# A copy buffer of its own for the final state, and reciprocal key norms spread by a product with the identity

## The chip, the core and the metric

The kernel runs on one core of a Trainium2 chip. The number that counts is device time in microseconds (us) of one execution. Before the change three runs gave 2194.7, 2196.6 and 2201.28 us, median 2196.6.

## What is computed

One inference step of a two-layer decoder: 512 prompt tokens and 8 x 4 sample tokens, model width 1024, 16 heads of 64. Layer 0 mixes time with an RWKV-7 recurrence, layer 1 with dilated window attention, and after each stands a gated feed-forward block. All arithmetic is float32; the large products are done as three products of split operands (a rounded part and its rest). Only the recurrence is touched by the change. Cut down to that, the reference is:

```python
kk = heads(k * k_k)
kk = kk / jnp.maximum(jnp.sqrt(jnp.sum(kk * kk, axis=-1, keepdims=True)), 1e-12)
k = k * (1.0 + (a - 1.0) * k_a)
y, S_T = wkv7_scan(rh, heads(decay), kh, vh, -kk, kk * ah, S0)
#   S = S * w + (S @ a) b^T + v k^T ;  y = S @ r      for each token
mean, var = jnp.mean(y, -1, keepdims=True), jnp.mean(jnp.square(y - mean), -1, keepdims=True)
y = ((y - mean) * lax.rsqrt(var + GN_EPS)).reshape(B, T, D) * ln_w + ln_b
bonus = jnp.sum(rh * kh * r_k, axis=-1, keepdims=True) * vh
out = ((y + bonus.reshape(B, T, D)) * g) @ w_o          # S_T, the last state, is an output too
```

## The kernel before

Tokens lie in two groups: group 0 has 288 columns (256 prompt tokens and the 32 sample tokens), group 1 the other 256. Channels lie in eight blocks `m` of 128, each with two heads; `jj` numbers pairs of blocks. The time mixing goes through these stages:

- Projections (`proj_gemm`, from L361): r, k and v. With k the sum of squares of every head and token is formed, and `rk[m]` holds its reciprocal root, one column for each head and block of 128 tokens.
- Preparation of group 0 (`unit_prep`, eight units), with the rest of the r and v projections beside it. In each unit `head_rows` (L126) turns the columns of `rk[m]` into rows: VectorE copies each column 64 times into `hr_e` (one buffer), TensorE transposes `hr_e` (three blocks for group 0, two for group 1; L135), and VectorE multiplies by the result (`kk`). A unit ends with its matrices `G`.
- `inverses`, nearly all VectorE, which waits for the `G` of all units.
- `chain` of group 0 (`scan(0)`), four steps that hand on the state `S`; beside it and after it the preparation of group 1 and the sample recurrences; then `inverses` of group 1.
- `chain` of group 1, whose four results are the tiles `yt`. Beside it the outputs of group 0: `y_norm` and `y_out`. `y_out` takes `bonus`, which lay in DRAM (`bonus_spill`), through the tile `bonus_in`, four buffers.
- `states` (L805): the last state is transposed in two halves, ScalarE copies each into `p_st`, and SyncE stores it to `o_p_wkv`. Then `y_norm` and `y_out` of group 1, and the products with `w_o` (`mm<-y`), where the rest of the kernel begins.

`p_st` carries the tag `y_sq`: it is the same single buffer in which `y_norm` puts the squares of each `yt`. Inside `y_norm` one tile goes through: sum (VectorE), mean taken off (VectorE), squares into `y_sq` (ScalarE), sum of squares `y_var` and its scaling (VectorE), power and product (GpSimd).

The program is written stage by stage, and a scheduler then places the instructions of all stages on each engine's queue; every engine works through its queue in order. So an instruction that waits holds everything behind it on its engine. Instructions issued through `Stream` all carry line 59 in the trace and are told apart by their tiles.

Of the kernel before, what the change touches and what calls it, by code (L numbers as in the profile page):

```python
# [9 lines left out]
F = mybir.dt.float32  # L10
# [11 lines left out]
NA = 288  # L22
# [7 lines left out]
def blocks(n):  # L30
    return (0, 128, 160) if n == NA else (0, 128)
# [41 lines left out]
def split(c, out_hi, out_lo, src, lo_engine, nc=None):  # L73
    (nc or c.nc).scalar.activation(out_hi, src, AF.Copy)  # L74
    lo_engine.tensor_tensor(out_lo, src, out_hi.bitcast(F), OP.subtract)  # L75
# [49 lines left out]

def head_rows(c, r, g, nc):  # L126

    e = c.lp.tile([128, 3, 128], F, name="hr_e", bufs=1)
    n = GRP[g][1]
    nb = len(blocks(n))  # L130
    nc.vector.tensor_copy(e[:, :nb].rearrange("p b (h k) -> p (b h) k", k=64),
                          r[:, 6 * g:6 * g + 2 * nb].unsqueeze(2).to_broadcast([128, 2 * nb, 64]))
    pr = c.pp()
    for j, at in enumerate(blocks(n)):
        nc.tensor.transpose(pr[:, at:at + 128], e[:, j, :], c.ident)  # L135
    return pr[:, :n]


# [251 lines left out]
def side_of(m):  # L390

    return (UP, LO) if m % 2 else (LO, UP)


def unit_prep(c, g, m, b, up, un, G, UV, bonus):
# [37 lines left out]
    if b:  # L433
        nc.gpsimd.memset(ds[:, :, 0:1], 1.0)
        nc.scalar.activation(ds[:, :, 1:5], s4(cl), AF.Exp, scale=-CDEC)
    prk = head_rows(c, c.rk[m], g, nc)
    kk = up.tile([128, NA], F, name="kk", tag="kk", bufs=c.ub)
    nc.vector.scalar_tensor_tensor(kk[:, :n], kS[:, :n], c.col("rwkv_k_k", m), prk, op0=OP.mult, op1=OP.mult)
# [284 lines left out]
def y_out(c, g, jj, yt, ys, yo, bonus, g2, y):  # L723

    nc, a = c.slow[3], c.a
    g0, n = GRP[g]
    pt = c.pp()
    for ch in range(4):
        nc.tensor.transpose(pt[:, 128 * ch:128 * ch + 128], yt[ch][:, 128 * jj:128 * jj + 128], c.ident)
    if g == 0:  # L730
        pk = c.sm()
        for par in range(2):
            x = 64 * ((2 * jj + par) % 4)
            for h in range(2):
                nc.tensor.matmul(pk[64 * h:64 * h + 64, 32 * par:32 * par + 32], ys[jj // 2][:, x:x + 64],
                                 c.pick[:, 32 * h:32 * h + 32], start=True, stop=True, tile_position=(0, 64 * h))
    for par in range(2):
        m = 2 * jj + par
        if bonus is None:
            bn = yo.tile([128, NA], F, name="bonus_in", bufs=4)  # L740
            nc.sync.dma_start(bn, c.bd[:, m])
        else:
            bn = bonus[:, m]
        bp = bn[:, 0:256].rearrange("p (c t) -> p c t", t=64)
        nc.vector.scalar_tensor_tensor(bp, pt.rearrange("p (c t) -> p c t", t=128)[:, :, side_of(m)[1]],
                                       c.col("rwkv_ln_w", m), bp, op0=OP.mult, op1=OP.add)
        if g == 0:
            nc.vector.scalar_tensor_tensor(bn[:, 256:NA], pk[:, 32 * par:32 * par + 32], c.col("rwkv_ln_w", m),
                                           bn[:, 256:NA], op0=OP.mult, op1=OP.add)
        ps = c.pp()  # L750
        nc.tensor.matmul(ps[:, :n], g2[:, m * 128:(m + 1) * 128], c.hg[:, g0:g0 + n], start=True, stop=True)
        t = yo.tile([128, NA], F, name="y_t", bufs=2)
        for src, to in ((slice(256, NA), slice(0, 32)), (slice(0, 256), slice(32, NA)))[g:]:
            to = slice(0, NB) if g else to
            nc.vector.scalar_tensor_tensor(t[:, to], bn[:, src], c.col("rwkv_ln_b", m), ps[:, src], op0=OP.add, op1=OP.mult)
        split(c, y[:, 0, m, :n], y[:, 1, m, :n], t[:, :n], nc.gpsimd, nc)


def rwkv(c, ctx, mx):

    nc, tc, a = c.nc, c.tc, c.a
    with ExitStack() as rx:
# [38 lines left out]
        def outputs(g):  # L801
            for jj in range(4):
                y_out(c, g, jj, st[g]["yt"], ysm, yo, bonus[g], g2, ys[g])

        def states(hb):  # L805
            pt = c.sm()
            for j in range(4):
                nc.tensor.transpose(pt[:, 128 * j:128 * j + 128], c.S[0][:, 4 * hb + j], c.ident)
            so = yo.tile([128, 4, 128], F, name="p_st", tag="y_sq", bufs=1)
            nc.scalar.activation(so, pt.rearrange("p (j k) -> p j k", j=4), AF.Copy)  # L810
            for h in range(2):
                q = slice(64 * h, 64 * h + 64)
                nc.sync.dma_start(a["o_p_wkv"][0, 0, 8 * hb + h:8 * hb + 8:2].rearrange("j v k -> v j k"), so[q, :, q])
# [98 lines left out]
        yo = rx.enter_context(c.pool("yo"))  # L912
# [13 lines left out]
        for hb in range(2):  # L926
            states(hb)
# [723 lines left out]
```

## Time and profile before

| | |
|---|---|
| median of the runs | 2196.6 us |
| the profiled execution | 2200.44 us |
| its span, first to last instruction | 2198.6 us |
| TensorE busy | 2020.5 us (92%) |
| VectorE busy | 1138.7 us (52%) |
| ScalarE busy | 879.1 us (40%) |
| GpSimd busy | 540.1 us (25%) |

TensorE's share is an average. It is close to full from about 520 us on, in the feed-forward blocks and the attention, and lower in the time mixing before that, where the engines wait for one another. The times below are of the profiled execution, counted from the start of its span.

### The profile page before, as it was taken

What the parts mean: (1) busy time and instruction counts of PE and PEld (TensorE: products, weight loads), DVE (VectorE), ACT (ScalarE), POOL (GpSimd) and SP (SyncE); (2) the same over time, 40 slices, a digit from 0 to 9 for tenths busy, and PEclk for the clock granted to TensorE, in tenths of its full rate; (3) what the DMA queues carried; (4) which work ended last, traced back from release to release, by engine and by line L of the source; (5) the groups of instructions that cost most, each with busy time, mean ns of one, the idle gap of its engine ahead of it and who ended that gap; (6) DMA issues with size and microseconds to landing.
All of it is one profiled execution on the core that took longest, in us unless ns stands there. A gap on an engine that the chain in (4) does not pass through costs nothing. (4 is left out here: it accounts for less than half of the span.)

```text
span 2198.6 us, 47990 instructions
## 1 busy us (share of the span) xinstructions
PE 2020.5 (92%) x19190; PEld 1893.1 (86%) x19190; DVE 1138.7 (52%) x2390; ACT 879.1 (40%) x1815; POOL 540.1 (25%) x680
## 2 busy tenths in 40 slices
PE   7998668487999999998999999999999989999998
PEld 6897556376899999998888988888898889999998
DVE  7647867865644343254554544545545553444323
ACT  5446435223544443243333333333334444444333
POOL 5525525254322221021111111111111132212001
PEclk9999879687999999999999999999999899999999
DMA  5266412313333233355444444444445332333323
GB/s 172 84 179 192 127 26 56 78 36 99 110 88 91 83 97 91 107 159 136 124 134 126 129 127 135 134 116 122 137 126 156 95 108 81 94 87 87 94 81 110
DMA packets 432379, 242.53 MB, mean 110 GB/s; under 512 B 40890, under 2 KB 424026, under 8 KB 432026
## 3 DMA queue, kind: packets, MB, share of 16 engines
q1 hardware_dynamic: 432154, 239.45, 38.5%
q8 instruction: 151, 2.47, 0.5%
q14 instruction: 74, 0.61, 0.1%
HBM read 198.42 MB, written 27.57 MB: 103 GB/s over the span
## 5 line engine op out<-in xcount | busy, mean ns | idle before, releaser
L98 PE MATMUL mm<-xn,w_hi 128*128 128x256 f32 (+1 forms) x2688 | 789.3, 294 | 0.0
L99 PE MATMUL mm<-xn,w_hi 128*128 128x256 f32 (+1 forms) x2688 | 786.3, 293 | 0.9 <-DVE xn L75 0.9
L100 PE MATMUL mm<-xn,w_lo 128*128 128x256 f32 (+1 forms) x2688 | 782.0, 291 | 0.0
L75 DVE TENSOR_TENSOR w_lo<-w_raw,w_hi 128x512 fp32r<-128x512 f32 (+1 forms) x575 | 431.8, 752 | 573.4 <-ACT w_hi L74 566.2
L74 ACT ACTIVATE w_hi<-w_raw 128x512 fp32r<-128x512 f32 (+1 forms) x575 | 355.9, 620 | 572.7 <-PE mm L99 506.1
L99 PEld LDWEIGHTS mm<-xn,w_hi 128*128 128x128 f32 x2688 | 511.5, 190 | 5.3 <-issue 2.8
L98 PEld LDWEIGHTS mm<-xn,w_hi 128*128 128x128 f32 x2688 | 510.4, 190 | 5.8 <-issue 0.4
L100 PEld LDWEIGHTS mm<-xn,w_lo 128*128 128x128 f32 x2688 | 510.6, 190 | 3.1 <-issue 3.0
L98 PE MATMUL mm<-act,w_hi 128*128 128x288 f32 (+1 forms) x704 | 201.2, 290 | 1.6 <-ACT y_out L1029 1.6
L99 PE MATMUL mm<-act,w_hi 128*128 128x288 f32 (+1 forms) x704 | 200.5, 289 | 0.0
L100 PE MATMUL mm<-act,w_lo 128*128 128x256 f32 (+1 forms) x704 | 199.4, 289 | 0.0
L1183 POOL TENSOR_TENSOR qk_raw<-qk_raw,rope 128x1088 f32<-128x1088 f32 x24 | 85.9, 3581 | 422.6 <-DMA qk_sw<-qk_raw 343.8
L98 PEld LDWEIGHTS mm<-act,w_hi 128*128 128x128 f32 x704 | 132.5, 190 | 1.7 <-ACT y_out L1029 1.7
L99 PEld LDWEIGHTS mm<-act,w_hi 128*128 128x128 f32 x704 | 132.3, 189 | 0.0
L100 PEld LDWEIGHTS mm<-act,w_lo 128*128 128x128 f32 x704 | 131.3, 189 | 0.0
L147 POOL TENSOR_TENSOR acc<-acc,sq_t 128x288 f32<-128x288 f32 (+1 forms) x56 | 46.1, 823 | 302.4 <-ACT sq_t L146 302.0
L98 PE MATMUL mm<-mx,w_hi 128*128 128x288 f32 (+1 forms) x384 | 113.0, 296 | 3.2 <-ACT p_out L371 1.6
L100 PE MATMUL mm<-mx,w_lo 128*128 128x288 f32 (+1 forms) x384 | 112.2, 295 | 1.7 <-DVE w_lo L75 1.7
L99 PE MATMUL mm<-mx,w_hi 128*128 128x288 f32 (+1 forms) x384 | 112.2, 293 | 0.0
L1268 ACT ACTIVATE scores<-scores,sm_m 128x512 f32<-128x512 f32 (+3 forms) x80 | 50.4, 631 | 71.5 <-DVE sm_m L1267 71.3
L98 PEld LDWEIGHTS mm<-mx,w_hi 128*128 128x128 f32 x384 | 73.3, 191 | 6.1 <-ACT w_hi L74 2.7
L100 PEld LDWEIGHTS mm<-mx,w_lo 128*128 128x128 f32 x384 | 73.1, 191 | 4.6 <-DVE w_lo L75 3.3
(334 smaller groups left out, 3036.5 us busy)
## 6 DMA issues: line engine op xcount, KB each, us to landing
w_raw<-ffn_w_up SPq DMA_DIRECT2D x176, 256.0 KB
w_raw<-attn_w_in SPq DMA_DIRECT2D x144, 256.0 KB
w_raw<-ffn_w_down SPq DMA_DIRECT2D x90, 256.0 KB
w_raw<-rwkv_w_rkv SPq DMA_DIRECT2D x80, 256.0 KB
qk_sw<-qk_raw SPq DMA_DIRECT2D x96, 136.0 KB
cache_k<-cache_k_w SPq DMA_DIRECT2D x96, 128.0 KB
cache_v<-cache_v_w SPq DMA_DIRECT2D x96, 128.0 KB
w_raw<-rwkv_w_o SPq DMA_DIRECT2D x32, 256.0 KB
```

What stands on the lines that cost most here:

```text
L74: (nc or c.nc).scalar.activation(out_hi, src, AF.Copy)
L75: lo_engine.tensor_tensor(out_lo, src, out_hi.bitcast(F), OP.subtract)
L98: nc.tensor.matmul(ps, hi, xhi(i), start=first and i == 0, stop=False)
L99: nc.tensor.matmul(ps, hi, xlo(i), start=False, stop=False)
L100: nc.tensor.matmul(ps, lo, xhi(i), start=False, stop=last and i == len(w) - 1)
L147: nc.gpsimd.tensor_tensor(acc, acc, t[:, :n], OP.add)
L1183: nc.gpsimd.tensor_tensor(raw, raw, c.rope[:, 0:1].to_broadcast([128, 2, NT]), OP.mult)
L1268: nc.scalar.activation(s[:, :w], s[:, :w], AF.Exp, scale=0.125, bias=m[:, 1:2], accum_out=m[:, 2:3])
```

## The change

`head_rows` no longer makes `hr_e`. For each block of 128 tokens and each of the two heads it issues one product, with the column of `rk[m]` read 64 times as the stationary operand and the identity as the moving one, into the 64 partitions of that head. The rows that come out are the same. `p_st` gets a buffer of its own (2 KB in each partition), and `bonus_in` goes from four buffers to two (1152 bytes each).

```diff
 def head_rows(c, r, g, nc):

-    e = c.lp.tile([128, 3, 128], F, name="hr_e", bufs=1)
     n = GRP[g][1]
-    nb = len(blocks(n))
-    nc.vector.tensor_copy(e[:, :nb].rearrange("p b (h k) -> p (b h) k", k=64),
-                          r[:, 6 * g:6 * g + 2 * nb].unsqueeze(2).to_broadcast([128, 2 * nb, 64]))
     pr = c.pp()
     for j, at in enumerate(blocks(n)):
-        nc.tensor.transpose(pr[:, at:at + 128], e[:, j, :], c.ident)
+        for h in range(2):
+            x = 6 * g + 2 * j + h
+            nc.tensor.matmul(pr[64 * h:64 * h + 64, at:at + 128], r[:, x:x + 1].to_broadcast([128, 64]), c.ident,
+                             start=True, stop=True, tile_position=(0, 64 * h))
     return pr[:, :n]
@@ y_out
-            bn = yo.tile([128, NA], F, name="bonus_in", bufs=4)
+            bn = yo.tile([128, NA], F, name="bonus_in", bufs=2)
@@ states
-            so = yo.tile([128, 4, 128], F, name="p_st", tag="y_sq", bufs=1)
+            so = yo.tile([128, 4, 128], F, name="p_st", bufs=1)
```

The scheduler orders the queues anew. From line 136 on, the changed file's line numbers are one less. At three places this is what stands on a queue before and after.

The first place is the end of the chain of group 1. ScalarE, before: the four `yt` tiles of group 1 are `yt_5279` to `yt_5282`, `cp` and `sm` are PSUM tiles, `y_5278` is the input of the products with `w_o`.

```order
L579 ACTIVATE yt_5281<-cp 128x512
L592 ACTIVATE W<-cp 128x256
L599 ACTIVATE UV<-cp 64x512
L579 ACTIVATE yt_5282<-cp 128x512
L810 ACTIVATE p_st<-sm 128x512 x2
L59 ACTIVATE y_sq<-yt_5279 128x512
L59 ACTIVATE y_sq<-yt_5280 128x512
L59 ACTIVATE y_sq<-yt_5281 128x512
L59 ACTIVATE y_sq<-yt_5282 128x512
L59 ACTIVATE y_5278<-y_t 128x256 x8
```

ScalarE at the same place, after; the four tiles are now `yt_5287` to `yt_5290`.

```order
L59 ACTIVATE y_sq<-yt_5287 128x512
L578 ACTIVATE yt_5289<-cp 128x512
L59 ACTIVATE y_sq<-yt_5288 128x512
L591 ACTIVATE W<-cp 128x256
L598 ACTIVATE UV<-cp 64x512
L59 ACTIVATE y_sq<-yt_5289 128x512
L578 ACTIVATE yt_5290<-cp 128x512
L809 ACTIVATE p_st<-sm 128x512
L59 ACTIVATE y_sq<-yt_5290 128x512
L809 ACTIVATE p_st<-sm 128x512
L59 ACTIVATE y_5286<-y_t 128x256 x8
```

Three of the four squares now stand among the last steps of the chain, and the fourth stands between the two state copies. VectorE's queue follows: after the change its rows between the state updates of the third and the fourth step (`S_3666`, `S_3665`) are these.

```order
L613 TENSOR_TENSOR S_3666<-cp,SD 64x8x64 x2
L59 SCALAR_TENSOR_TENSOR yt_5287<-y_sum,yt_5287 128x512
L59 TENSOR_REDUCE y_sum<-yt_5288 128x8
L59 TENSOR_REDUCE y_var<-y_sq 128x8
L59 TENSOR_SCALAR y_var<-y_var 128x8
L59 SCALAR_TENSOR_TENSOR yt_5288<-y_sum,yt_5288 128x512
L590 COPY W<-cp 128x256
L59 TENSOR_REDUCE y_sum<-yt_5289 128x8
L59 TENSOR_REDUCE y_var<-y_sq 128x8
L59 TENSOR_SCALAR y_var<-y_var 128x8
L59 SCALAR_TENSOR_TENSOR yt_5289<-y_sum,yt_5289 128x512
L597 COPY UV<-cp 64x512
```

Behind the last of these stand one more `y_var` with its scaling and then `S_3665`. Before the change one `y_sum` and the two copies `W` and `UV` were all that stood between the two updates.

The second place is SyncE's queue of DMA issues from the end of the preparation on, before and then after.

```order
L914 DMA g_5011<-rwkv_g 128x1024
L741 DMA bonus_in<-bonus_spill 128x288 x4
L701 DMA o_s_wkv<-st 64x4x64 x16
L86 DMA w_raw<-rwkv_w_o 128x4x128 x8
L741 DMA bonus_in<-bonus_spill 128x288 x4
L955 DMA x<-x_spill 128x544 x3
```

```order
L913 DMA g_5019<-rwkv_g 128x1024
L740 DMA bonus_in<-bonus_spill 128x288 x2
L700 DMA o_s_wkv<-st 64x4x64 x16
L86 DMA w_raw<-rwkv_w_o 128x4x128 x8
L740 DMA bonus_in<-bonus_spill 128x288 x6
L954 DMA x<-x_spill 128x544 x3
```

Two loads of `bonus_in` go early instead of four, and six wait in line for a buffer instead of four.

The third place is GpSimd at the last unit of group 0's preparation, before and then after; `th_3117` and `th_3124` are that unit's tile `th`, and `st` is work for the sample recurrences, which come later.

```order
L59 TENSOR_TENSOR BE<-BK,dc 128x512
L59 MEMSET dx 128x4
L59 TENSOR_TENSOR st<-s_BK_2021,s_dend_2025 128x128 x2
L59 TENSOR_TENSOR s_BK_2028<-tk,di 64x8x4
L59 TENSOR_TENSOR st<-s_BK_2021,s_dend_2025 128x128 x2
L59 TENSOR_TENSOR s_BK_2028<-th_2948,di 64x8x4
L59 TENSOR_SCALAR s_V_2030<-in_2952 64x8x4
L59 TENSOR_TENSOR tk<-in_3120,tk 128x288
```

```order
L59 TENSOR_TENSOR BE<-BK,dc 128x512
L59 TENSOR_TENSOR s_BK_2028<-tk,di 64x8x4
L59 TENSOR_TENSOR s_BK_2028<-th_2954,di 64x8x4
L59 TENSOR_SCALAR s_V_2030<-in_2958 64x8x4
L59 TENSOR_TENSOR tk<-in_3127,tk 128x288
L59 TENSOR_TENSOR th_3124<-kk,th_3124 128x288
```

The four `st` products have left this place; they now stand behind the last unit.

## Rows read from the trace of the kernel before

**Rows 1.** The page's first line: span and instructions.

```profile
span 2198.6 us, 47990 instructions
```

**Rows 2.** Windows: start:end, length, busy us (instructions) by engine, TensorE clock, DMA.

```profile
165.00:265.00 100.00, 81.91 (x672) 72.48 (x672) 80.57 (x149) 61.05 (x144) 61.35 (x109) 0.95 0.61 175
...
489.00:520.10 31.10, 10.09 (x39) 7.17 (x40) 12.37 (x28) 6.69 (x13) 14.54 (x13) 0.62 0.26 80
520.10:2198.60 1678.50, 1628.24 (x15131) 1554.42 (x15129) 773.78 (x1681) 651.75 (x1306) 303.90 (x376) 0.98 0.40 113
```

**Rows 3.** Timeline, 488 to 521 us: start, duration, instruction, [idle before <-releaser].

```profile
488.92 0.60 ACT L579 ACTIVATE yt<-cp 128x512 f32<-128x512 f32 x1 [3.15 <-PE cp L577]
489.95 0.60 ACT L810 ACTIVATE p_st<-sm 128x512 f32<-128x512 f32 x1 [0.43 <-PE sm L808]
494.46 0.60 ACT L810 ACTIVATE p_st<-sm 128x512 f32<-128x512 f32 x1 [3.91 <-DMA o_p_wkv<-p_st]
499.72 0.63 ACT L59 ACTIVATE y_sq<-yt 128x512 f32<-128x512 f32 x1 [4.67 <-DMA o_p_wkv<-p_st]
500.38 0.69 DVE L59 TENSOR_REDUCE y_var<-y_sq 128x8 f32<-128x512 f32 x1 [11.18 <-ACT y_sq L59]
501.42 1.94 POOL L59 TENSOR_TENSOR y_var<-y_var,mhalf 128x8 f32<-128x8 f32 x1 [16.87 <-DVE y_var L59]
510.88 2.04 POOL L59 TENSOR_TENSOR yt<-yt,y_var 128x512 f32<-128x512 f32 x2
520.15 0.49 PE L98 MATMUL mm<-y,w_hi 128*128 128x288 f32 x1
```

**Rows 4.** The last state update, and the window between it and the one before.

```profile
482.28:487.80 5.52, 4.22 (x102) 3.78 (x100) 1.81 (x5) 1.57 (x3) 2.11 (x2) 1.00 0.00 0
487.80 1.41 DVE L614 TENSOR_TENSOR S<-cp,SD 64x512 f32<-64x512 f32 x2 [1.97 <-PE cp L607]
```

**Rows 5.** Timeline of VectorE, 464 to 478 us: outputs of group 0 beside the chain.

```profile
464.65 0.64 DVE L59 SCALAR_TENSOR_TENSOR y_t<-bonus_in,par,pp 128x32 f32<-128x32 f32 x2
466.50 0.88 DVE L59 SCALAR_TENSOR_TENSOR bonus_in<-pp,par,bonus_in 128x256 f32<-128x256 f32 x2 [0.32 <-PE pp L729]
469.78 1.39 DVE L614 TENSOR_TENSOR S<-cp,SD 64x512 f32<-64x512 f32 x2 [0.75 <-PE cp L607]
474.82 0.63 DVE L59 SCALAR_TENSOR_TENSOR y_t<-bonus_in,par,pp 128x32 f32<-128x32 f32 x2
477.31 0.88 DVE L59 SCALAR_TENSOR_TENSOR bonus_in<-pp,par,bonus_in 128x256 f32<-128x256 f32 x2
```

**Rows 6.** Timeline: a load of 144 KB issued by SyncE, and who waited for it.

```profile
191.22 0.43 SPq L411 DMA_DIRECT2D in<-rkv_spill  x1
195.10 0.60 PE L446 MATMUL pp<-ca,in 128*64 128x128 f32 x4 [0.89 <-DMA in<-rkv_spill]
```

**Rows 7.** Windows with the instructions of `hr_e` alone: PE, PEld and DVE busy.

```profile
165.00:265.00 100.00, 4.25 (x24) 2.77 (x24) 4.02 (x8) 0.95 0.61 175
265.00:400.00 135.00, 3.36 (x16) 1.74 (x16) 2.80 (x7) 0.87 0.18 42
```

**Rows 8.** Timeline, 248 to 252 us: last unit of group 0's preparation.

```profile
248.51 1.32 POOL L59 TENSOR_TENSOR st<-s_BK,s_dend 128x128 f32<-128x128 f32 x2
250.00 0.75 POOL L59 TENSOR_TENSOR st<-s_BK,s_dend 128x128 f32<-128x128 f32 x2
251.12 0.50 ACT L59 ACTIVATE th<-pp,hpar 128x288 f32<-128x288 f32 x1 [2.86 <-POOL s_BK L59]
```

**Rows 9.** Timeline of TensorE: two transposes, eight products, and what starts behind each.

```profile
345.52 0.41 PE L135 MATMUL pp<-ca,hr_e 128*128 128x128 f32 x2
345.76 0.60 PE L446 MATMUL pp<-ca,in 128*64 128x128 f32 x4
...
320.16 1.09 PE L573 MATMUL cp<-S,AR 128*64 128x128 f32 x16
321.08 1.10 PE L577 MATMUL cp<-UV,G 128*64 128x64 f32 x32
```

## The prediction

> **What bounds the kernel now.** I read the page first: the span [rows 1], and the shares, where TensorE is busy for 92% of it. Then I cut the span into stages by windows [rows 2]. From 520.10 us to the end TensorE is busy 1628.24 of 1678.50 us; the change touches nothing there, its queues keep their order there, so whatever is won or lost before 520 us is kept to the end. The time mixing ahead of it is bound otherwise. The window 489.00 to 520.10 us is the emptiest: TensorE 10.09 of 31.10 us, no engine above half. The timeline of that window names the reason [rows 3]. The chain's last result leaves ScalarE at 488.92 + 0.60 = 489.52. ScalarE then copies half of the state, waits 3.91 us until that half is stored, copies the other half, and waits 4.67 us for the second store, because the squares of the norm use the same buffer. Only at 499.72 does the norm of group 1 go on, and VectorE and GpSimd sit behind it (11.18 and 16.87 us idle). The four tiles leave GpSimd at 510.88 + 2.04 = 512.92, and 7.2 us later, at 520.15, the products with w_o start. The preparation of group 0, 165 to 265 us, is shared: TensorE 81.91 and VectorE 80.57 of 100 us [rows 2], and its end is VectorE's, since the inverse needs all units.
>
> **The state copies.** In the new order three tiles are squared during the chain and the fourth right behind the first state copy, ahead of any store. What is left between the last yt (489.52) and the last tile's leaving GpSimd is one tile's own way: sum, mean off, sum of squares at 0.69 each, squares 0.63, a small scaling (about 0.2, an estimate from the gap between 500.38 + 0.69 and 501.42), power 1.94, product 2.04 / 2 = 1.02 [rows 3]: 2.07 + 0.63 + 0.2 + 1.94 + 1.02 = 5.9 us, where 512.92 - 489.52 = 23.4 us went by. That is 17.5 us less. Is anything else late then? The second state copy still waits 3.91 us for the first store, and the eight y copies stand behind it on ScalarE. The first copy ends 1.03 us after the last yt (490.55 to 489.52); with 3.91 and 0.60 the second ends 5.5 us after it. The first y copy needs the last tile (5.9) and then two VectorE steps and a transpose, some 1.9 us more; so the copy is out of the way 2 us early, and I cost that wait at nothing. If the store took over 2 us longer, every further us would show.
>
> **What the chain pays for it.** VectorE worked 1.81 us in the 5.52 us between the last two state updates [rows 4]. Now eight steps of 0.69 and three scalings of 0.2 stand there in place of one step of 0.69: 1.81 - 0.69 + 5.5 + 0.6 = 7.2 us, 1.7 longer than the gap. They partly wait for ScalarE's squares, and the copies W and UV, which the chain's products wait for, are queued behind them. The mean of the first tile, though, now stands behind the earlier update and not ahead of it, which brings that update forward by up to 0.69. I take 2.0 us, from 1.1 (1.7 less 0.6) to 2.8 (the two waits for squares, 0.63 each, fully in the way and 0.1 for the rest).
>
> **Two buffers for bonus_in.** The load for block 3 can go only when block 1 has been read, at 464.65 + 0.64 = 465.29, and is wanted at 466.50 + 0.44 = 466.94 [rows 5]: 1.65 us. The nearest row is a load of the same 144 KB, waited for from 191.22 to 195.10, 3.88 us [rows 6], with the DMA engines busy. Then 2.2 us are missing; VectorE is in order, the chain's state update is queued behind, and 0.75 us idle ahead of it cover part: 1.5 us lost at most. The load for block 6 goes at 474.82 + 0.63 = 475.45 and is wanted at 477.31: 2.0 us missing, nothing idle behind it. Block 2 and 7 lie in the shadow of these, blocks 4 and 5 have over 5 us. So 0 to 3.5 us; the queues are nearly empty there (4 loads), so I take 2.2.
>
> **head_rows, VectorE.** The copies into hr_e go: 4.02 us in 165 to 265, 2.80 us later [rows 7]. With VectorE busy for eight tenths of the first stage, and one copy directly ahead of its last G, I count 3.2 of the 4.02; bounds 0 and 4.0. In the later stage, chains of waits over all engines, I count 1.4 of 2.8.
>
> **head_rows, TensorE.** 40 transposes become 80 products (6 and 4 in a unit). Two transposes hold TensorE for 345.76 - 345.52 = 0.24, 0.12 each; eight products with 64 stationary and 128 moving columns, in 16 records, for 321.08 - 320.16 = 0.92, 0.115 each [rows 9]. A unit pays 6 x 0.115 - 3 x 0.12 = 0.33 us in group 0, 0.22 in group 1: 2.6 and 1.8 us in all. TensorE does not set the end of either stage; I count 1.0 and 0.9.
> The Trainium skill (FP8 and Floating Point Precision, TensorE Precision Notes) says that a true FP32 product takes four passes through the array, and its page TensorE: Matmul & The Clock Gate (Terms) calls the transpose mode four times as fast for FP32. By that a product is 4 x 0.12 = 0.48 and not 0.115, and the rows above speak against it.
>
> **Order at the end of the first preparation.** ScalarE waited 2.86 us for GpSimd in the last unit, which did two pairs of st, 1.32 and 0.75 us [rows 8]; both are now placed later. I count 2.0, bounds 0 and 2.9. The scheduler also sets the preparation ahead of the projections and spreads those to the last unit. VectorE's 19.4 idle us are what this can fill or widen; I count 0, from 3 lost to 6 won.
>
> **Sum.** 17.5 - 2.0 - 2.2 = 13.3 at the end; 3.2 - 1.0 + 2.0 = 4.2 in group 0's preparation; 1.4 - 0.9 = 0.5 in group 1's. In all 18.0 us: the profiled execution's 2200.44 (span 2198.6 and 1.84 around it) becomes 2182.4. The median lies 3.84 below that execution, so the prediction is 2196.6 - 18.0 = 2178.6.
>
> **Rivals.**
> *The norm isn't early after all.* The squares stand early in the queue, but each tile's sum, mean, squares and sum of squares (2.7 us) hold VectorE and ScalarE in order, and the chain's W and UV wait behind all three tiles: 8.1 us instead of 2.0. With nothing won in the preparation: 17.5 - 8.1 - 2.2 = 7.2, so 2189.4. Against it: only parts of each tile stand ahead of W and of UV. Chance 0.08.
> *The loads bite.* Both late loads take 3.88 us or more and the chain pays 2.8: 17.5 - 2.8 - 3.5 = 11.2, and nothing in the preparation: 2185.4. Chance 0.12.
> *The preparation fills up.* The new order uses VectorE's idle time for 6 us more, and the rest holds: 24 us, 2172.6. For it: the idle time lies mostly in the last two units, where projection work now stands. Chance 0.15.
> *Slower.* Products with the identity cost TensorE far more than the rows of other products say, in both preparations, where six tenths and more of its time are taken. The gains without their cost are 13.3 + 3.2 + 2.0 + 1.4 = 19.9; so slower from 80p - 4.8 = 19.9, p = 0.31 us a product, and past the bound below from 0.39. The dearest product in the rows, the first mm<-y with 0.49 us for 288 columns [rows 3], is the bound from above: 80 x 0.49 - 4.8 = 34.4 against 19.9, 14.5 us slower: 2211.1. That holds only if all of it lies on the path, and the nearest rows show 0.115. Chance 0.03. By the rule of the Trainium skill named above, 0.48 a product, it would be 2210.3.
>
> **How the numbers follow.** The forecast has 0.62. About 0.3%, 6.6 us, is what a measurement of this kernel can tell from no change. The first rival lies at that edge; I give half of it to no change, with 0.02 from a forecast whose parts all fall short: same 0.06. Slower is its rival and 0.01 more, 0.04. Faster 0.90. Downwards the range takes the third rival and the low ends of chain and loads (0.9 + 2.2), less than all at once: 2168. Upwards the second rival and a few us of reordering, and one more unknown: TensorE's granted clock is 0.62 on the mean of the window that shrinks [rows 2], and w_o's first products may meet the low level; some 1.5 us either way. 2190.
>
> **What would show it.** Right: in the changed profile no wait of y_sq for o_p_wkv, and the first mm<-y some 14 us sooner after the inverse of group 1 than before; the preparation of group 0 over some 4 us sooner than before; the stretch from mm<-y to the end again 1678 us. The state update behind block 3 or 6 waits for a DMA if the loads bite. It is wrong if VectorE's copies W and UV start over 5 us later than their products end, if the six products of a unit take over 1 us, or if the preparation ends later than before.

## The result, and the profile after

The changed kernel takes 2184.24 us (median of six runs, 2182.79 to 2190.87) where the kernel before took 2197.08 beside it: a ratio of 0.9947, 95% interval 0.993 to 0.9964. That is 12.8 us less; the forecast was 2178.6, 18.0 us less, with a range of 2168 to 2190. The direction and the range held, and three tenths of the gain is missing. The traced execution took 2183.52 us against 2200.44.

Windows of the changed kernel, which answer to [rows 2]; columns as there (start:end, length, busy us of TensorE, its weight loads, VectorE, ScalarE and GpSimd with their instructions, TensorE's clock, DMA share, GB/s):

```profile
165.00:265.00 100.00, 85.58 (x728) 75.01 (x726) 74.52 (x140) 59.54 (x140) 63.65 (x109) 0.97 0.53 158
495.40:509.48 14.08, 7.71 (x31) 6.07 (x30) 8.05 (x18) 4.30 (x9) 6.67 (x9) 0.64 0.58 178
509.48:2181.70 1672.22, 1625.91 (x15131) 1551.51 (x15129) 773.44 (x1681) 651.90 (x1306) 304.42 (x375) 0.98 0.40 113
```

The second line is the stretch from the last yt to the first product with w_o: 14.08 us, and 520.15 - 489.52 = 30.63 before [rows 3]. Cut at the same five events, the two traces differ so:

| stretch | before | changed | difference | forecast |
|---|---|---|---|---|
| start to the last G of group 0 | 264.58 | 262.85 | -1.7 | -4.2 |
| from there to the first yt of group 1 | 192.66 | 195.03 | +2.4 | -0.5 |
| first yt to the end of the last | 32.28 | 37.52 | +5.2 | +4.2 |
| from there to the first product with w_o | 30.63 | 14.08 | -16.5 | -17.5 |
| from there to the end | 1678.45 | 1672.22 | -6.2 | 0 |

The last line is not the change's: a second trace of the changed kernel has 1681.02 us there and a second one of the kernel before 1675.35. Up to the first product with w_o the pair differs by 10.7 us.

The tail went as forecast. Timeline of the changed kernel (start, duration, engine, line, operation, [idle before <-releaser]):

```profile
494.80 0.60 ACT L578 ACTIVATE yt<-cp 128x512 f32<-128x512 f32 x1 [3.65 <-PE cp L576]
495.48 0.60 ACT L809 ACTIVATE p_st<-sm 128x512 f32<-128x512 f32 x1
496.93 0.63 ACT L59 ACTIVATE y_sq<-yt 128x512 f32<-128x512 f32 x1 [0.86 <-DVE yt L59]
500.35 1.04 POOL L59 TENSOR_TENSOR yt<-yt,y_var 128x512 f32<-128x512 f32 x1
500.49 0.60 ACT L809 ACTIVATE p_st<-sm 128x512 f32<-128x512 f32 x1 [2.93 <-DMA o_p_wkv<-p_st]
503.26 0.81 ACT L59 ACTIVATE y<-y_t 128x256 fp32r<-128x256 f32 x2 [2.18 <-DVE y_t L59]
509.48 0.48 PE L98 MATMUL mm<-y,w_hi 128*128 128x288 f32 x1
```

No square waits for a store any more. The last tile leaves GpSimd at 500.35 + 1.04 = 501.39, 5.99 us after the last yt (495.40); the forecast was 5.9. The second state copy still waits for the first store, and ends 2.17 us before the first y copy starts.

The chain paid for it. VectorE of the changed kernel between the second state update of group 1 and the last, which answers to [rows 4, 5]:

```profile
465.93 0.25 DVE L59 SCALAR_TENSOR_TENSOR bonus_in<-sm,par,bonus_in 128x32 f32<-128x32 f32 x1 [0.99 <-DMA bonus_in<-bonus_spill]
470.67 0.25 DVE L59 SCALAR_TENSOR_TENSOR bonus_in<-sm,par,bonus_in 128x32 f32<-128x32 f32 x1 [1.37 <-DMA bonus_in<-bonus_spill]
478.03 0.48 DVE L59 SCALAR_TENSOR_TENSOR bonus_in<-pp,par,bonus_in 128x256 f32<-128x256 f32 x1 [0.58 <-DMA bonus_in<-bonus_spill]
480.49 0.48 DVE L59 SCALAR_TENSOR_TENSOR bonus_in<-pp,par,bonus_in 128x256 f32<-128x256 f32 x1 [1.05 <-DMA bonus_in<-bonus_spill]
482.42 1.38 DVE L613 TENSOR_TENSOR S<-cp,SD 64x512 f32<-64x512 f32 x2
486.00 0.60 DVE L59 TENSOR_SCALAR y_var<-y_var 128x8 f32<-128x8 f32 x1
487.22 0.42 DVE L590 COPY W<-cp 128x256 f32<-128x256 f32 x1
488.87 0.97 DVE L59 TENSOR_SCALAR y_var<-y_var 128x8 f32<-128x8 f32 x1
490.46 0.69 DVE L597 COPY UV<-cp 64x512 f32<-64x512 f32 x1
491.97 0.17 DVE L59 TENSOR_SCALAR y_var<-y_var 128x8 f32<-128x8 f32 x1
492.98 1.39 DVE L613 TENSOR_TENSOR S<-cp,SD 64x512 f32<-64x512 f32 x2 [0.84 <-PE cp L606]
```

Four waits for loads, 4.0 us in all, and then a last step of 10.6 us between updates (482.42 to 492.98) where there were 6.9 before (480.90 to 487.80). W starts 3.42 us after the update ended; before it was 1.2 (483.48, the update over at 482.28):

```profile
483.48 0.42 DVE L591 COPY W<-cp 128x256 f32<-128x256 f32 x1 [0.48 <-PE cp L588]
```

On TensorE, in the changed kernel:

```profile
487.70 1.66 PE L595 MATMUL cp<-W,G 64*64 64x64 f32 x32 [2.75 <-DVE W L590]
489.86 0.48 PE L728 MATMUL pp<-ca,yt 128*128 128x128 f32 x1 [0.51 <-POOL yt L59]
490.13 1.72 PE L750 MATMUL pp<-hg,g 128*128 128x256 f32 x4
491.78 1.15 PE L606 MATMUL cp<-UV,BT 128*64 128x64 f32 x32
```

Here are two things that the prediction hadn't looked for. TensorE idles 2.75 us for W, and its products run long afterwards (1.66 us for 32 records, 1.15 at the high clock). And the first products of group 1's outputs, L728 and L750, stand in TensorE's queue ahead of L606, which the state update waits for: UV is there at 491.15, L606 starts at 491.78. The clock, in windows of 2 us of the same kernel:

```profile
484.50:486.50 2.00, 0.45 (x10) 0.21 (x4) 1.90 (x4) 1.11 (x2) 1.93 (x2) 1.00 0.00 0
486.50:488.50 2.00, 0.80 (x20) 0.80 (x22) 1.97 (x5) 0.90 (x2) 1.83 (x2) 0.90 0.00 0
488.50:490.50 2.00, 1.50 (x19) 1.28 (x17) 1.93 (x4) 0.59 (x1) 1.82 (x3) 0.50 0.00 0
490.50:492.50 2.00, 2.00 (x28) 1.39 (x28) 1.51 (x3) 0.63 (x1) 1.92 (x2) 0.74 0.01 4
```

The granted clock goes from 1.0 (2.4 GHz) to 0.5 (1.2 GHz) after a stretch in which TensorE was busy for 0.45 of 2 us, inside the chain. In the kernel before it stayed at 1.0 from 467 us up to the last yt.

### The profile page after: what moved, and what is told of

Its sections match the earlier page's. It is cut to its first block, busy times and chain, and to the rows that moved or that the text cites. A ratio compares the mean times of both kernels' runs of the same rounds, so it can differ in the third digit from the quotient of the medians.

```text
span 2181.7 us, 48234 instructions
## 1 busy us (share of the span) xinstructions
PE 2030.3 (93%) x19310; PEld 1900.0 (87%) x19310; DVE 1132.3 (52%) x2374; ACT 879.3 (40%) x1815; POOL 544.7 (25%) x680
```

## The experiments

Each row is one trace, so the kernel before, the changed kernel and e9 have two. The stages, in us: the end of the last G of group 0; in the chain of group 0 the time between the first two updates of S; from the last of these updates to the end of the last G of group 1; the three steps between the yt of group 1; and the tail from the last yt to the first product with w_o. Under "heads" stands how `head_rows` spreads the norms in the units of group 0 and of group 1: T are transposes, P products.

| kernel | heads | last G, 0 | S1 to S2 | to last G, 1 | yt steps | tail |
|---|---|---|---|---|---|---|
| before | T T | 264.58 | 9.35 | 59.66 | 15.34 9.83 6.51 | 30.63 |
| e12 (before again) | T T | 265.51 | 9.35 | 63.01 | 13.87 9.84 6.51 | 30.93 |
| changed | P P | 262.85 | 10.73 | 60.09 | 15.02 12.25 9.65 | 14.08 |
| e0 (changed again) | P P | 266.59 | 10.70 | 60.16 | 15.33 12.56 10.60 | 13.40 |
| e1 copies, 2 loads | T T | 265.87 | 9.36 | 59.81 | 15.29 13.70 11.63 | 13.57 |
| e2 products only | P P | 263.94 | 10.74 | 60.19 | 15.34 9.83 6.51 | 30.83 |
| e3 loads only | T T | 263.97 | 9.99 | 65.01 | 15.37 11.63 7.98 | 30.90 |
| e4 changed, 4 loads | P P | 264.15 | 10.60 | 60.05 | 15.32 9.83 12.25 | 13.55 |
| e9 and W, UV first | P P | 264.55 | 10.23 | 58.78 | 14.99 9.84 7.46 | 15.29 |
| e14 (e9 again) | P P | 263.90 | 10.74 | 60.22 | 13.77 9.83 7.47 | 14.52 |
| e11 copies, 4 loads | T T | 266.28 | 9.78 | 65.15 | 15.34 9.83 12.28 | 13.56 |
| e10 and W, UV first | T T | 265.56 | 9.35 | 62.98 | 15.34 9.84 9.00 | 13.48 |
| e13 as e9, mixed | P T | 260.76 | 9.37 | 68.23 | 14.09 9.93 10.13 | 14.73 |
| e5 products twice | P P | 268.56 | 11.76 | 63.10 | 9.20 10.04 10.13 | 15.11 |

**The parts.** Three kernels each make one part of the change, and one makes all of it, on one chip.

e1: `p_st` without the tag, `bonus_in` with two buffers, `head_rows` as before.

```diff
-            bn = yo.tile([128, NA], F, name="bonus_in", bufs=4)
+            bn = yo.tile([128, NA], F, name="bonus_in", bufs=2)
-            so = yo.tile([128, 4, 128], F, name="p_st", tag="y_sq", bufs=1)
+            so = yo.tile([128, 4, 128], F, name="p_st", bufs=1)
```

> Only the state copies' own buffer and two buffers for bonus_in; the key norms are still spread by hr_e and transposes. By the sum of the prediction: 17.5 - 2.0 - 2.2 = 13.3 us faster than the kernel before. By the stages of the changed kernel's trace: last yt to first product with w_o 30.63 - 14.08 = 16.5 us shorter, first yt to last yt 36.92 - 31.68 = 5.2 us longer, so 11.3 us faster. Rival: the gain of the changed kernel comes in part from the products; then this one gains under 9 us.

Measured: 2196.56 us against 2203.38, ratio 0.996 (0.9937 to 0.9983), 6.8 us faster. The tail is 17.1 us shorter, and the chain of group 1 pays 8.9 (41.2 for 32.3), more than the 5.2 of the first trace: 8.2 us won by its stages. The interval reaches from 3.7 to 13.9 us, so the time allows the 11.3 expected and the rival's under 9 alike.

e2: the new `head_rows` alone.

> Only the products with the identity in head_rows; state copies and bonus_in as before. By the sum of the prediction: 4.2 + 0.5 = 4.7 us faster. By the stages of the changed kernel's trace: 1.7 us won up to the last G of group 0, and 2.4 us lost again between there and the first yt of group 1, so 0.6 us slower, no difference that can be measured. Rival: the products cost more than they spare in both preparations; over 3 us slower.

Measured: 2203.70 against 2203.38, ratio 0.9993 (0.9975 to 1.0011): nothing that can be told from no change; the interval goes from 5.5 us faster, which would hold the 4.7 forecast, to 2.4 slower. Its chain of group 1 and its tail are those of the kernel before to 0.2 us.

e3: `bonus_in` with two buffers alone.

> The kernel before with two buffers for bonus_in in place of four, nothing else. By the prediction's term: 2.2 us slower (0 to 3.5). By the changed kernel's trace: second yt to third yt of group 1 took 12.25 us where it took 9.83, so 2.4 us slower, in that stretch alone. Rival: the chain of group 1 waits for something else there anyway, 0.

Measured: 2206.85 against 2203.38, ratio 1.0008 (0.9989 to 1.0027), so by the time it can't be told from none. By the stages the loads cost 1.8 us in the second step of the yt and 1.5 in the third. Another 5.4 us between the last S and the last G of group 1 come with TensorE's clock, below.

e0: all of it, that is the changed kernel.

> The changed kernel itself beside its parts on one chip. If the parts add up, it is faster than the kernel before by the gain of the copies alone plus that of the products alone, within 2 us; the stages of its trace say 11.3 - 0.6 = 10.7 us, the prediction said 18.0. Rival: the parts disturb or help one another and the sum is off by more than 3 us.

Measured: 2188.56 against 2203.38, ratio 0.9921 (0.9894 to 0.9947), 14.8 us faster. The copies alone gave 6.8 and the products alone nothing, so the medians don't add up, by 8 us; the intervals are about 5 us to either side in each, and taken together they just allow that.

**The chain of group 1.** Four buffers for `bonus_in` and the new `p_st` fit together, since `hr_e` is gone.

e4: the changed kernel with `bufs=4` for `bonus_in`.

> The changed kernel with four buffers for bonus_in again. If the two buffers cost what the trace says, the step from the second to the third yt of group 1 goes from 12.25 back to about 9.8 us and the step from the third to the fourth stays near 9.7; 2 to 4 us faster than the changed kernel, some 10 to 13 us faster than the kernel before by the stages. Rival: norm steps fill what the loads leave, and the two steps together stay over 20 us.

Measured: 2187.11 against 2204.16, ratio 0.9927 (0.9909 to 0.9946). The second step is back at 9.83, so the 2.4 us there are the loads'. But the third grew from 9.65 to 12.25: the two take 22.08 together, and 21.90 with two buffers. The rival was right, and by the time e4 can't be told from the changed kernel (0.9947 and 0.9921). The windows of e4 from its third yt on show where it went:

```profile
483.81:485.81 2.00, 1.02 (x16) 0.78 (x16) 1.97 (x3) 0.60 (x1) 1.93 (x2) 1.00 0.04 8
485.81:487.81 2.00, 0.73 (x22) 0.73 (x24) 1.97 (x5) 0.90 (x2) 1.83 (x2) 1.00 0.00 0
487.81:489.81 2.00, 1.06 (x18) 0.92 (x16) 1.96 (x3) 0.59 (x1) 1.81 (x3) 0.59 0.00 0
489.81:491.81 2.00, 2.00 (x12) 1.17 (x13) 1.55 (x3) 0.63 (x1) 1.63 (x2) 0.50 0.01 4
491.81:493.81 2.00, 2.00 (x38) 2.00 (x36) 0.44 (x1) 0.00 (x0) 2.00 (x2) 0.50 0.00 0
```

VectorE is busy without a gap for 6 us with the norm steps, TensorE for under half of that, and then it works for 6 us and more at 0.5. In e4 L606 took 1.98 us and not 1.15.

e9: e4, and in the last step the norm steps stand behind the copies that TensorE waits for (`add_manual_dep` gives the scheduler an order and adds no work). The sum of tile 1 is placed behind W and that of tile 2 behind UV, the sum of squares of tile 0 behind W and that of tile 1 behind UV.

```diff
-        nc.vector.tensor_copy(W[:, 0:256], w[:, 0:256])
+        c.step = [nc.vector.tensor_copy(W[:, 0:256], w[:, 0:256]).ins]
...
-        nc.vector.tensor_copy(UV[UP, ch, 0, :], pu[0][UP])
+        c.step.append(nc.vector.tensor_copy(UV[UP, ch, 0, :], pu[0][UP]).ins)
...
-        nc.vector.reduce_sum(s, t, axis=AX.X)
+        r = nc.vector.reduce_sum(s, t, axis=AX.X)
+        if len(yt) == 4 and i in (1, 2):
+            c.tc.add_manual_dep(r.ins, c.step[i - 1].name,
...
-        nc.vector.reduce_sum(var, sq[:, :k], axis=AX.X)
+        r = nc.vector.reduce_sum(var, sq[:, :k], axis=AX.X)
+        if len(yt) == 4 and i < 2:
+            c.tc.add_manual_dep(r.ins, c.step[i].name,
...
```

> As the run with four buffers, and in the last step of the chain the copies W and UV stand ahead of the norm steps that are not needed yet (order only: the first tile's sum of squares and the second tile's sum behind W, the third tile's sum behind UV). If the norm steps in front of W and UV make the last step long, it goes from 9.65 to under 7.5 us, and the stretch from the last yt to the first product with w_o grows by less than 1 us from about 14: 2 us faster than with four buffers alone. Rival: the length is TensorE's and ScalarE's, and the step stays over 9 us; or the tail pays it back in full.

Measured: 2183.59 against 2204.16, ratio 0.9916 (0.9901 to 0.9931), 20.6 us faster than the kernel before. The third step takes 7.46 and the tail 15.29, 1.7 longer than in e4 and not under 1; from the first yt to w_o it is 48.2 us where e4 took 51.6. TensorE's rows for W and UV in e9, and the window of its third yt step:

```profile
483.87 1.15 PE L595 MATMUL cp<-W,G 64*64 64x64 f32 x32 [0.53 <-DVE W L590]
486.71 1.15 PE L606 MATMUL cp<-UV,BT 128*64 128x64 f32 x32 [1.69 <-DVE UV L597]
```

```profile
482.33:489.79 7.46, 5.12 (x128) 4.61 (x128) 6.09 (x11) 2.73 (x5) 6.24 (x5) 1.00 0.01 2
```

The wait for W is 0.53 us, where it was 2.75 in the changed kernel and 2.25 in e4, and the clock stays at 1.0.

e14: e9 once more.

> The fastest kernel so far once more, beside the one before it in this list on one chip: products in both groups, four buffers, W and UV first. About 18 us faster than the kernel before if the first measurement holds (0.9916, 0.9901 to 0.9931); last G of group 1 within 61 us of the last state update of group 0's chain, its clock at the high level there.

Measured: 2184.80 against 2203.66, ratio 0.991 (0.989 to 0.993); the steps repeat to 0.01 us, but for the first.

**Are the products needed?** e11 keeps transposes and moves `hr_e` into the buffers of the preparation, so that four buffers for `bonus_in` and the new `p_st` fit without the products; e10 is e11 in the order of e9.

```diff
-    e = c.lp.tile([128, 3, 128], F, name="hr_e", bufs=1)
+    e = up.tile([128, 3, 128], F, name="hr_e", bufs=1)
-            so = yo.tile([128, 4, 128], F, name="p_st", tag="y_sq", bufs=1)
+            so = yo.tile([128, 4, 128], F, name="p_st", bufs=1)
```

> The state copies' own buffer alone: transposes and hr_e stay, but hr_e lies in the buffers of the preparation, which are given up before the outputs, so that bonus_in keeps four buffers. If the products with the identity bring nothing, this is the whole gain: tail 16.5 to 17 us shorter, last step of the chain 3 us longer, 13 to 14 us faster than the kernel before, and 2 to 4 us more than the changed kernel's own stages give. Rival by the prediction's sum: 17.5 - 2.0 = 15.5 faster, and 4.7 less than with the products and four buffers.

Measured: 2191.30 against 2204.16, ratio 0.9946 (0.9934 to 0.9958), 12.9 us faster.

> As the run before, and W and UV ahead of the norm steps in the last step of the chain. If every reading so far holds this is the fastest of all: 15 to 16 us faster than the kernel before by the stages. Rival: the order gives nothing (same as the run before).

Measured: 2191.79 against 2204.16, ratio 0.9948 (0.9932 to 0.9964). By the time the order gives nothing here, though from the first yt to w_o e10 takes 48.3 us and e11 51.6, the same 3.4 us less as e9 against e4. Its third step is 9.00 where e9's is 7.46:

```profile
486.90:495.90 9.00, 6.79 (x129) 6.34 (x130) 7.56 (x13) 2.83 (x6) 7.70 (x6) 0.81 0.02 5
```

TensorE waits for W and for UV as long as in e9, 0.53 and 1.69 us, and the last two updates of S lie 8.38 us apart in both, and the queues have the same order in this step. But e10's clock is at 0.5 from 491.4 to 494.8 us. So the fall costs 1.5 us here, and it came without the long wait for W.

The counterparts with products, e4 and e9, are 4 and 8 us faster on the same chip; e4's interval overlaps that of e11, and e9's ends where that of e10 begins. Between S1 and S2 the kernels with products are 0.8 and 0.9 us slower. The stage that pays for the transposes is the one from the last S to the last G of group 1: 65.15 and 62.98 us, with products 60.05 and 58.78.

e13: e9, but units of group 1 take `hr_e` and transposes again.

> As the run with four buffers and W and UV first, but group 1's units take hr_e and transposes again (group 0 keeps the products). If the products lengthen the first step of group 0's chain, beside which group 1's first units stand, the stretch between its first two state updates goes from 10.2 to 10.7 us back to about 9.4, and by the stages this kernel is 1 to 2 us faster than the same with products in both groups. Rival: TensorE has less to do in the last units of group 1, its granted clock falls there (as in two of four runs with transposes, from 384 us on, the last G of group 1 then 3 to 5 us later), and it is 2 to 6 us slower.

Measured: 2188.61 against 2203.66, ratio 0.9936 (0.9916 to 0.9957), 3.8 us slower than e14 on the same chip, with intervals that overlap. S1 to S2 is 9.37 again, so the longer stretch goes with the products in group 1's units; how much of it they cost stands below. And the last G of group 1 comes 68.23 us after the last S. Windows of e13 from 370 us:

```profile
370.00:375.00 5.00, 5.00 (x62) 3.87 (x61) 1.69 (x4) 2.69 (x6) 0.78 (x2) 1.00 0.04 14
375.00:380.00 5.00, 2.70 (x16) 1.92 (x15) 4.93 (x8) 2.75 (x8) 5.00 (x6) 0.92 0.00 0
380.00:385.00 5.00, 5.00 (x26) 4.26 (x25) 3.02 (x5) 0.00 (x0) 3.00 (x5) 0.50 0.00 0
```

and TensorE's row in it, ahead of which it stood idle:

```profile
377.84 0.67 PE L478 MATMUL pp<-pb,ca 128*128 128x256 f32 x2 [2.19 <-ACT di L59]
```

The same row of the changed kernel, and its window:

```profile
381.63 0.67 PE L472 MATMUL pp<-pb,ca 128*128 128x256 f32 x2 [0.46 <-DVE pb L59]
```

```profile
380.00:385.00 5.00, 4.43 (x38) 3.36 (x34) 5.00 (x9) 2.40 (x6) 5.00 (x5) 1.00 0.00 0
```

In the order that the transposes bring, TensorE waits 2.19 us for ScalarE there, and in e3, e11 and e13 its clock then falls to 0.5 for 14 to 24 us. The same 2.19 us stand in both traces of the kernel before, in e1 and in e10, and no fall follows them; in the first trace of the kernel before the clock is at 1.0 all through:

```profile
340.00:398.00 58.00, 51.23 (x396) 38.20 (x395) 45.95 (x77) 32.98 (x78) 37.77 (x48) 1.00 0.30 70
```

The third yt step of e13 is 10.13 us although its clock is 1.0 there, and so is that of e5 below. In both a square of the norm stands ahead of the last yt on ScalarE and waits 3.0 us for VectorE, while the last two updates of S are 8.9 us apart. The yt steps of two kernels compare cleanly only where the queues have the same order, as those of e9 and e10.

e12: the kernel before, one more trace.

> The kernel before, one more trace. Between the last state update of group 0's chain and the last G of group 1 the first trace shows 59.7 us at the high clock; two of four kernels with transposes showed 65.0 and 65.2 with a clock of 0.5 from 385 us on. If that fall belongs to the transposes' order and not to the other edits, this one may show it too; 59 to 60 us would leave it open.

Measured: 63.01 us, 3.3 more than in the first trace of the same kernel. Here the fall comes sooner, behind a wait of 1.36 us at 349.6, and so it does in e10:

```profile
350.00:360.00 10.00, 10.00 (x50) 6.87 (x49) 8.17 (x14) 4.96 (x12) 5.62 (x8) 0.66 0.43 90
```

So over all traces this stage took 59.7 to 68.2 us with transposes in group 1 (seven traces, five of them 62.98 or more, mean 63.4), and 58.8 to 60.2 with products once each (six traces, mean 59.9). The products' order isn't free of falls: TensorE waits 2.06 us ahead of L472 at 348 us, and in five of the six traces, the changed kernel's among them, some 3 us at 0.5 follow:

```profile
348.00:352.00 4.00, 4.00 (x17) 2.42 (x17) 1.74 (x4) 0.60 (x1) 2.61 (x5) 0.57 0.56 116
```

The length of the stage goes with its time at 0.5. With transposes it takes 59.7 and 59.8 us without any (before, e1), 63.0 with 7 us of it (e12, e10), 65.0 and 65.2 with 14 (e3, e11) and 68.2 with 24 (e13); with products 58.8 without any (e9) and 60.1 to 60.2 with 3. So where the clock holds the products' order is some 1 us better, by one trace, and the rest of its advantage goes with the shorter time at 0.5.

**What a product costs.** e5 issues every product of `head_rows` twice.

```diff
-        for h in range(2):
+        for h in (0, 1, 0, 1):
```

> The changed kernel with every product of head_rows issued twice, the second over the first (160 in place of 80, same result). At 0.134 to 0.145 us each (changed trace) that is 11 us more of TensorE. By the prediction TensorE sets the end of neither preparation: under 3 us slower than the changed kernel. Rival: they lie on the path, 8 to 11 us slower, and the first step of group 0's chain is another 1.3 us longer.

Measured: 2191.66 against 2203.66, ratio 0.9941 (0.9918 to 0.9964); beside the changed kernel's 0.9947 and 0.9921 no difference shows in the time. The stages answer better: the last G of group 0 at 268.56, 4.7 us later than the mean of the seven traces with single products in group 0 (263.8, from 260.76 to 266.59); S1 to S2 1.0 us longer; from the last S to the last G of group 1 3.0 longer. That is 8.7 us for 80 products at the most: some 2.3 of the 4.7 stand ahead of the first G, which comes at 191.7 and on the mean of the seven at 189.4 (191.8 in e0), and the 3.0 come with 7 us at the low clock where the changed kernel has 3. What was lost came back in the first step of group 1's chain, 9.20 for 13.8 to 15.4 us: in this order TensorE hardly idles there, and its clock stays at 1.0. In each of the other thirteen traces TensorE waits 2.2 to 2.8 us for the update of S in that step, and its clock falls to 0.5.

## Why the prediction was right, and where its steps missed

**The tail held.** A tile's own way was forecast at 5.9 us and took 5.99, in the copies-only kernels too (5.99 and 6.06). The wait of the second copy costs nothing, with 2.17 us to spare where 2 were forecast. What lies behind it took 0.9 us more than before (8.09 from the last tile to w_o against 7.23), which the sum didn't have.

**The norm steps in the chain were sized too low.** 2.0 us was taken, between 1.1 and 2.8. The third yt step grew by 3.1 us in the changed kernel and by 4.1 in its second trace; with the loads out of the way by 5.7. Three parts were missing. A scaling was put at 0.2 us; two of three took 0.60 and 0.97. The order was read on ScalarE, VectorE and SyncE, not on TensorE, where L728 and L750 stand ahead of L606 (0.6 us). And no term stood for TensorE's clock: its fall alone is worth 1.5 us between e9 and e10. e9, which moves the norm steps behind W and UV, has the step at 7.46 with the clock at 1.0, and 3.4 us less than e4 from the first yt to w_o. That the wait for W brought the fall isn't shown, since e10 has the fall without that wait. The first rival (the norm's steps in W's and UV's way, up to 8.1 us) came closer than its 0.08 said: 3.1 to 5.7 lies between it and the forecast.

**The loads were sized right, for another reason and in part by luck.** 2.2 us forecast, 2.4 in the second step; the other traces with two buffers have 2.7 (e0), 3.9 (e1), 1.8 and 1.5 more in the third step (e3), and 0.2 (e5) there. A load is faster than the bound taken from [rows 6]: the loads issued at 463.74 and 468.39 were waited for until 465.93 and 470.67, 2.2 and 2.3 us, not 3.88; but the waits fall on blocks 2, 4, 6 and 7, where 3 and 6 were named. SyncE's issues of the first load and of the third and fourth, in the changed kernel:

```profile
463.74 0.34 SPq L740 DMA_DIRECT2D bonus_in<-bonus_spill  x1
...
468.39 1.25 SPq L740 DMA_DIRECT2D bonus_in<-bonus_spill  x2
```

Two of the four waits lie in the first yt step, which did not grow (15.02 for 15.34). Nor is the load a term by itself: without the loads' wait the chain loses as much to the norm steps (e4).

**The preparation of group 0 gained less.** 4.2 us forecast. The last G came at 263.8 on the mean of seven traces with single products and at 265.3 on that of six with transposes, 1.5 us, while two traces of one kernel differ by up to 3.7. VectorE did get rid of the copies (74.52 us busy of 100 for 80.57 before). The end of the stage went as read: the 2.86 us that ScalarE waited for GpSimd in the last unit are 0.16 in the changed kernel.

```profile
249.31 0.50 ACT L59 ACTIVATE th<-pp,hpar 128x288 f32<-128x288 f32 x1 [0.16 <-POOL s_BK L59]
```

From the G of the sixth unit to the last G the seven traces with products take 11.9 to 12.8 us, the six with transposes 15.7 to 16.8. But from the first unit's G to the sixth's they take 61.0 to 63.3 us, with transposes 56.8 to 58.0, although VectorE has less to do. The prediction had no term for that loss of some 5 us, and no run separates its cause. The step that the runs speak against is "TensorE does not set the end of either stage": e5 takes as long as the others up to the sixth unit (62.3) and 14.6 us for the last two, 2.3 more, with 12 products more in them. So the loss ahead of the sixth unit isn't the products' own time, and at the end TensorE's time does count, by one trace. And the price was low: six products hold TensorE for 0.80 us there, 0.134 each, not 0.115.

**Between the preparations two effects were missed.** Ahead of the second state update of group 0's chain stand eight products of group 1's first two units. From the last G of group 0 to that update the six traces with products take 56.2 us on the mean, the seven with transposes 55.2. That is 1.0 us for two units, where the prediction had 0.9 for all eight of group 1. The 0.9 to 1.4 us between S1 and S2 are not all the products': from the copy W to S2 it is 7.14 us for 6.66, and the rest lies ahead of W, where e3 and e11 lose 0.4 to 0.7 with transposes too. In the changed kernel:

```profile
301.25 1.12 PE L133 MATMUL pp<-ca,rk 128*64 128x128 f32 x8
302.30 1.80 PE L637 MATMUL sm<-ca,vk 128*128 128x128 f32 x8
...
313.08 0.66 PE L133 MATMUL pp<-ca,rk 128*64 128x128 f32 x8
313.66 0.41 PE L445 MATMUL pp<-ca,in 128*64 128x128 f32 x2
```

The first four hold TensorE for 1.05 us, still at the low clock after the inverses, the next four for 0.58 at the high one; two transposes took 0.28 and 0.22 in the same places, both at the high clock. Against that stands the second effect, the clock in the rest of group 1's preparation, 3.5 us on the mean. It was in no view of the one trace of before, whose clock happened not to fall there; so this gain is luck as far as the prediction goes.

**The sum.** Of the 18.0 us the stages of the pair show 10.7 and the medians 12.8 and 14.8. That the medians show more than the pair fits the clock in group 1's preparation, which the first trace of before did not lose and others did; since each kernel was traced once or twice, that this is the whole difference isn't shown. The forecast's range held because the large term was right; its small gains in the preparation (4.7) were not there in the pair, where the last G of group 1 comes at 398.22 and 398.61. Over all traces it comes 2.6 us sooner (399.5 on the mean of the six with products in both groups, 402.1 on that of the six with transposes in both), by the clock and not by the terms of the forecast.

**A better kernel.** e9 is the fastest measured: 2183.59 and 2184.80 us, ratios 0.9916 and 0.991, against 0.9947 and 0.9921 of the changed kernel. The intervals touch, so the rest of the time hides the gain; from the first yt of group 1 to w_o the gain over the changed kernel's 51.6 is 3.4 and 5.4 us, 1.2 of the latter in the first step, which the order doesn't touch.

## What to carry to other kernels

When a wait goes and work moves forward into a chain of small steps, look for the copies on which the next engine waits, and let nothing stand ahead of them that isn't needed yet: here such steps made the chain's last step 3 to 6 us longer, and an order alone won 3.4 us back. Read the new order on every engine of the chain, TensorE too. And where a stage's length depends on the clock, one trace shows one draw: cost it from two traces at least, or put a fall into the range.

## What the hardware showed that was not expected

TensorE's granted clock fell to 0.5 in some executions and not in others behind the same row. The wait of 2.19 us in group 1's preparation stands in seven traces: a fall follows in three (14 to 24 us at 0.5) and none in the other four. Behind the 2.06 us of the products' order it fell in five of six, for some 3 us, and behind the 1.36 us at the same place in the transposes' order in two of six, for some 7. Nothing tried here decides which execution falls.

The scaling of eight numbers in each partition (y_var) takes 0.17 us on VectorE, and 0.60 and 0.97 where a GpSimd product was running. It ends with that product. GpSimd in the changed kernel:

```profile
483.88 1.56 POOL L602 TENSOR_TENSOR SD<-S,dc 64x512 f32<-64x512 f32 x1 [0.50 <-DVE S L613]
485.51 1.06 POOL L602 TENSOR_TENSOR SD<-S,dc 64x512 f32<-64x512 f32 x1
...
488.76 1.04 POOL L59 TENSOR_TENSOR yt<-yt,y_var 128x512 f32<-128x512 f32 x1
```

485.51 + 1.06 = 486.57 and 486.00 + 0.60 = 486.60; 488.76 + 1.04 = 489.80 and 488.87 + 0.97 = 489.84. The sums of VectorE beside these products kept their 0.68 to 0.69. It goes the other way round too: the first of the two SD products started 0.05 us behind VectorE's product at 483.83, which kept its 0.69, and took 1.56 us where the second took 1.06. The Trainium skill (SBUF — State Buffer, SBUF: two separate sides) tells of a port pair that VectorE and GpSimd share under an exclusive lock, which the one that comes second waits for; these rows agree.
